# A two-layer transformer forward pass on one core: the norm between sublayers in three held steps, three late output tiles by stream, the softmax scaling inside the turning matmul, and one block's low part by an accumulating DMA

## The chip, the cores and the metric

The kernel runs on one core of one Trainium2 chip. The metric is device time in microseconds (us) of one execution; lower is better. Times of a kernel are given as the median of several runs with the lowest and the highest. A profiled execution gives the trace, with the start and the length of every instruction on the engines: PE (TensorE's matmuls), PEld (its weight loads), DVE (VectorE), ACT (ScalarE), POOL (GpSimd) and SP, which issues DMAs.

## The reference: what is computed

Two token streams of 256 tokens and width 1024, the latents and the context, go through two layers; in layer 1 the context serves only as keys and values, and the result is the latents alone. Cut to what matters:

```python
def _modulate(t, g, shift, scale):
    return _rms(t, g) * (1 + scale) + shift
def _swiglu(h, w13, w2):
    gte, up = jnp.split(h @ w13, 2, axis=-1)
    return (jax.nn.silu(gte) * up) @ w2
for i in range(2):            # layer 0 mixes by convolution, layer 1 by attention
    mod = (silu(c) @ mod_w[i] + mod_b[i])         # 9 vectors: shift, scale, gate of 3 sublayers
    lat = lat + 0.5 * gate * _swiglu(_modulate(lat, ...), ffn_w13[i, 0], ffn_w2[i, 0])
    y = _short_conv_mixer(h, ...) or _gqa_mixer(h, hc, ...)     # of the modulated norm
    lat = lat + gate * y
    lat = lat + 0.5 * gate * _swiglu(_modulate(lat, ...), ffn_w13[i, 1], ffn_w2[i, 1])
```

The hidden width of the ffn is 2816. Attention has 8 query heads and 2 key/value heads of width 128, with an RMS norm and a rotary embedding on queries and keys; 256 queries see 512 keys (context, then latents). The context stream goes through the same steps up to layer 1's keys and values. Everything is float32.

## The kernel before

**Layout.** Activations lie transposed: 8 tiles (`m` or `k`) of 128 features by 512 token columns, 256 of each stream (`S` = 256, `T2` = 512). `s` = 0 is the latents, `s` = 1 the context. A product keeps float32's accuracy by parts: `split` (line 91) makes a high part by an ACT copy to fp32r and a low part by a DVE subtraction, and `mm3` (112 to 118) issues three matmuls: high·high, high·low, low·high. Weights come as 1 MB tiles `wr` over SP's queue (`load_raw`, 86, three buffers), and are split into `wh` and `wl` (four buffers of 128x1024 each).

**Order.** A framework schedules each engine's instructions at build time by its own estimates and by the program's order, inserts the waits, and gives buffers from pools by name. An instruction passed through `tc.keep_in_program_order` stays, on its engine, behind everything that the program had written before it.

**FFN.** `ffn` (600) goes over the hidden tiles in three parts of 8, 7 and 7, and after each part `project` (454) multiplies by `w2` and adds to the residual `x` (`finish`, line 438, with the gate). Most column tiles of `w13` are done by `Pair` (525): a scheme of 7 block products in place of 8, in which the weight blocks A11, A12, A22 and the sums S1 to S4 meet the activations' blocks B and their sums T1 to T4 (`Blocks.sums`, 314). One pair is 7 products x 4 `k` x 3 matmuls = 84 matmuls of 256 columns. `head` does A11 and A12 (these need the first stream's norm only), `five`, `six`, `seven` and `four` the rest; `four` is the product of A22 with T4, whose weights are `w4h` and `w4l` (128x512, two buffers; split at line 561). In the first ffn of layer 0 some tiles are done plainly.

**The norm between sublayers.** `project` computes the output tiles in order; the last two (`late` = 2) are done for stream 0 first, then for stream 1, so that one stream's norm can run while the other is still being projected. `tail_norm` (386) runs with each tile: `square_add` (208) sums the squares; after the last tile `rms_inv` (226) sums over the partitions with four small matmuls (line 231), takes the root (ACT) and the reciprocal `ri` (DVE, line 240), and spreads it over the partitions with two 128x128 matmuls against the identity (line 242). Then `rest` makes the normed and modulated activations, first half of the features and then the second (lines 250, 304 and the split into `bh`, `bl`; or `norm_k` with `hh`, `hl` for a plain layout). These steps wait in a list, `pending`, and `flush` (381) runs them at places in the next stage's code. For stream 0 there are two steps, for stream 1 one, which also makes T1 to T4. The four projections with late tiles by stream are the ends of the first ffn of layer 0, of the convolution's `cw_out`, of the second ffn of layer 0, and of the first ffn of layer 1.

**The next stage after a norm** starts with stream 0: in `ffn` one plain tile's first 256 columns (`pg`, `pu`), the heads of two pairs (`p`, `q`), then the same tile's columns of stream 1. In the convolution (811 to 849) the first tile `m` = 0 goes by stream, 24 products each.

**Modulation.** The 18 x 8 tiles of the modulation vectors are dot products on DVE (`junk`, line 136: 128x1024 custom operations; 236 of them). They are done as filler: `tick(n)` (173) owes `n` units and issues whole ones, each 1 MB block of `modT` serving up to four; `mod_ready` (180) issues all that are still missing.

**Attention (908 to 1085).** `q_proj`, `k_proj` and `v_proj` with norms and the rotary part between; `scores` (1007) forms for each head two tiles of 128 queries by 512 keys, their maximum `mx`, the exponentials `e` with their sum (ACT, 1024), the reciprocal `r` (1028) and `pn` = e·r (DVE, 1032). `turn` (1036) transposes `pn` by matmuls against the identity (1041) and splits the result to `pth`, `ptl`; `mix` (1052) multiplies by the values. Then `project` with `wo`, the last norm, and the last ffn for the latents alone.

Of the kernel before, what the change touches and what calls it, by code (L numbers as in the profile page):

```python
# [39 lines left out]
def hybrid_kernel(ctx: ExitStack, tc: tile.TileContext, a: dict, out: bass.AP):  # L40
# [70 lines left out]

    def mm3(ps, w, m, first, last, more=False):
        wh, wl = w
        mh, ml = m
        kw = {"skip_group_check": True} if more else {}
        nc.tensor.matmul(ps, wh, mh, start=first, stop=False, **kw)  # L116
        nc.tensor.matmul(ps, wh, ml, start=False, stop=False, **kw)  # L117
        nc.tensor.matmul(ps, wl, mh, start=False, stop=last, **kw)  # L118
# [107 lines left out]
    def rms_inv(s, parts):  # L226

        pq = psmall("ss")
        for i in range(2):
            for n, t in enumerate(parts):  # L230
                nc.tensor.matmul(
                    pq[:, S + i : S + i + 1], t[:, i * P : i * P + P], ones[:, 0:1],
                    start=(n == 0), stop=(n == len(parts) - 1),
                )
# [5 lines left out]
        nc.vector.reciprocal(ri, rs)  # L240
        for i in range(2):
            nc.tensor.matmul(
                pq[:, i * P : i * P + P], ri[:, i : i + 1].to_broadcast([P, P]), ident,
                start=True, stop=True,
            )
# [38 lines left out]
    class Blocks:  # L284
# [29 lines left out]
        def sums(self):  # L314
# [8 lines left out]
            tt(out=b11, in0=b12, in1=b11, op=ALU.subtract)  # L323
            keep("T1", b11)
            tt(out=b12, in0=b22, in1=b12, op=ALU.add)
            tt(out=b22, in0=b22, in1=b11, op=ALU.add)
            keep("T2", b22)
            tt(out=b21, in0=b21, in1=b22, op=ALU.subtract)
            keep("T3", b12)
            keep("T4", b21)  # L330
# [50 lines left out]
    def flush(n=9):  # L381
        while pending and n:
            pending.pop(0)()
            n -= 1

    def tail_norm(l, j, h):
# [3 lines left out]
        def tail(m, c0, c1):  # L390
            square_add(m, c0, c1)
            if m == KT - 1:
# [5 lines left out]
                def inv():  # L398
                    return rms_inv(s, (accs[s], accs[s, "last"]))

# [8 lines left out]
                def both_parts():  # L409
                    ri = inv()  # L410
                    for part in range(2):
                        rest(part, ri)
                    if isinstance(h, Blocks):
                        h.sums()

                if s == 0:
                    keep = []

                    def one():
                        keep.append(inv())  # L420
                        rest(0, keep[0])

                    pending.append(one)
                    pending.append(lambda: rest(1, keep[0]))
                    if (l, j) == (1, 2):
                        flush()
                else:
                    flush()
                    pending.append(both_parts)
# [24 lines left out]
    def project(ws, src, nk, gate, tail, tot, late, ev, between=()):  # L454
# [42 lines left out]
        if late:  # L497

            wl = [get(m) for m in (6, 7)]
            if tail:  # L500
                ready()
            for s in range(2):
# [22 lines left out]
    class Pair:  # L525
# [6 lines left out]
        def __init__(self, src, h):  # L532
            self.h = h
            raw = load_raw(src)
            a21, a22, a11, a12 = (raw[:, i * T2 : i * T2 + T2] for i in range(4))
            tt = nc.vector.tensor_tensor
            sm = wp.tile([P, 2048], F32, name=nm("ws"), tag="ws", bufs=1)
            s1, s2, s3, s4 = (sm[:, i * T2 : i * T2 + T2] for i in range(4))
            self.w = {}

            def keep(keys, src):
                hi, lo = half()
                split(hi, lo, src)
                for i, key in enumerate(keys):
                    self.w[key] = [t[:, i * T2 : i * T2 + T2] for t in (hi, lo)]

            keep(("A11", "A12"), raw[:, 1024:])
            tt(
# [618 lines left out]
```

## Time and profile before

| what | value |
|---|---|
| median of 3 runs | 1613.26 us (1612.75 to 1616.25) |
| the profiled execution | 1611.37 us |
| its span in the trace | 1609.5 us |
| mean granted TensorE clock | 0.992 |
| DMA traffic | 248.77 MB |

How to read the rows. A group's row gives line, engine, operation, out<-in by the program's names, partitions x elements and type, the count, then busy us, mean ns of one, and the engine's idle time ahead of the group with what ended it. A row of the windows gives a stretch of time, then for each engine its busy us and the number of instructions that ran in it, the granted TensorE clock (1 is full speed), the mean busy share of the 16 DMA engines, and GB/s. A row of the waits gives engine, operation and line, what it waited for, the total, the number of times and the longest. A row of the timeline gives start and length; a wait stands in brackets. A row of the DMA issues gives the count, the size and the median time from issue to landing. TensorE's matmuls are pipelined, so the length of one is more than its share of the time; what a window holds tells the rate.

### The profile page before, as it was taken

Reading aid. Unit: us, or ns where it says so; the run is one execution under the profiler, and the core shown is the slowest. Engines: PE = TensorE matmul, PEld = TensorE weight load, DVE = VectorE, ACT = ScalarE, POOL = GpSimd, SP = SyncE. Lnnn points to the kernel's source line nnn. Section 1 sums busy time; section 2 is a strip of 40 time slices with the busy share of each in tenths; the row PEclk is TensorE's granted clock in tenths of the full one; section 3 lists DMA queues with packets and bytes.
Section 4 is the critical chain, followed back from the end, with each engine's and each line's share of the span. In section 5 each row is a group of like instructions: output and inputs, shape, how many; then the busy total and the mean of one; then the engine's idle time right before and its main releaser. Section 6 shows DMA issues by size and latency. Waiting matters only on the chain.

```text
span 1609.5 us, 25613 instructions
## 1 busy us (share of the span) xinstructions
PE 1576.1 (98%) x10566; PEld 1450.1 (90%) x10566; DVE 1332.4 (83%) x2035; ACT 722.2 (45%) x1110; POOL 0.2 (0%) x4
## 2 busy tenths in 40 slices
PE   9999999999999999999999999999999999899999
PEld 6788998999888889899899889889899897789999
DVE  4988778879998889799797999898898789965554
ACT  5532452544322365335255465245254455454443
POOL 0000000000000000000000000000000000000000
PEclk9999999999999999999999999999999999999999
DMA  8456235234565513353433413452432463755453
GB/s 320 162 183 209 80 122 180 90 135 152 177 221 186 180 41 117 132 183 100 168 120 115 154 54 131 172 195 96 156 129 96 180 214 108 270 201 185 169 194 109
DMA packets 38277, 248.77 MB, mean 155 GB/s; under 512 B 5136, under 2 KB 6928, under 8 KB 12304
## 3 DMA queue, kind: packets, MB, share of 16 engines
q1 hardware_dynamic: 35712, 245.38, 43.7%
q10 hardware_dynamic: 2448, 1.76, 0.4%
q8 instruction: 82, 1.34, 0.3%
q14 instruction: 35, 0.29, 0.1%
HBM read 244.77 MB, written 1.05 MB: 153 GB/s over the span
## 4 chain that ended last, share of the span: by engine, by line
PE 82%; DVE 12%; DMA 3%; ACT 2%; issue 1%; DVEq 0%; ACTq 0%; SPq 0%
PE py L117 7%; PE py L116 7%; PE py L118 7%; PE p L116 6%; PE p L118 6%; PE p L117 6%; PE q L118 5%; PE q L116 5%; PE q L117 5%; DVE junk L136 4%; DVE wl L93 3%; PE pg L117 2%; PE pg L118 2%; PE pg L116 2%; PE pu L117 2%; PE pu L118 2%
## 5 line engine op out<-in xcount | busy, mean ns | idle before, releaser
L92 ACT ACTIVATE wh<-wr 128x1024 fp32r<-128x1024 f32 (+2 forms) x274 | 274.4, 1014 | 395.0 <-PE py L117 108.7
L93 DVE TENSOR_TENSOR wl<-wr,wh 128x1024 fp32r<-128x1024 f32 (+2 forms) x274 | 318.2, 1167 | 97.0 <-ACT wh L92 96.4
L136 DVE CUSTOM_DVE_ANT_0 junk<-wr,scbc,modb 128x1024 bf16<-128x1024 f32 x236 | 302.5, 1282 | 39.6 <-DMA wr<-in_modT 37.0
L117 PE MATMUL py<-gl,wh 128*128 128x512 f32 (+1 forms) x746 | 263.2, 353 | 0.0
L116 PE MATMUL py<-gh,wh 128*128 128x512 f32 (+1 forms) x746 | 263.1, 353 | 0.0
L118 PE MATMUL py<-gh,wl 128*128 128x512 f32 (+1 forms) x746 | 262.9, 352 | 0.0
L93 DVE TENSOR_TENSOR wl<-ws,wh 128x1024 fp32r<-128x1024 f32 x112 | 136.8, 1223 | 27.3 <-ACT wh L92 27.0
L118 PEld LDWEIGHTS py<-gh,wl 128*128 128x128 f32 x746 | 141.1, 189 | 19.1
L116 PEld LDWEIGHTS py<-gh,wh 128*128 128x128 f32 x746 | 141.2, 189 | 18.6
L117 PEld LDWEIGHTS py<-gl,wh 128*128 128x128 f32 x746 | 141.2, 189 | 18.0
L92 ACT ACTIVATE wh<-ws 128x1024 fp32r<-128x1024 f32 x112 | 117.8, 1057 | 76.4 <-PE p L117 34.2
L116 PE MATMUL p<-th,wh 128*128 128x256 f32 x448 | 126.8, 283 | 0.0
L117 PE MATMUL p<-tl,wh 128*128 128x256 f32 x448 | 126.8, 283 | 0.0
L118 PE MATMUL p<-th,wl 128*128 128x256 f32 x448 | 126.6, 283 | 0.0
L117 PE MATMUL q<-bl,wh 128*128 128x256 f32 x336 | 95.2, 283 | 0.0
L116 PE MATMUL q<-bh,wh 128*128 128x256 f32 x336 | 95.1, 283 | 0.0
L118 PE MATMUL q<-bh,wl 128*128 128x256 f32 x336 | 95.1, 283 | 0.0
L438 DVE SCALAR_TENSOR_TENSOR x<-py,G,x 128x256 f32<-128x256 f32 x168 | 74.2, 480 | 21.4 <-PE py L118 21.2
L116 PEld LDWEIGHTS p<-th,wh 128*128 128x128 f32 x448 | 86.0, 192 | 0.5 <-ACT sg L584 0.2
L117 PEld LDWEIGHTS p<-tl,wh 128*128 128x128 f32 x448 | 86.0, 192 | 0.3
L118 PEld LDWEIGHTS p<-th,wl 128*128 128x128 f32 x448 | 85.9, 192 | 0.0
L116 PE MATMUL pg<-hh,wh 128*128 128x256 f32 (+1 forms) x240 | 75.8, 316 | 4.6 <-ACT hh L260 4.6
(236 smaller groups left out, 4001.3 us busy)
## 6 DMA issues: line engine op xcount, KB each, us to landing
wr<-in_w SPq DMA_DIRECT2D x88, 1024.0 KB, 4.9
wr<-in_modT SPq DMA_DIRECT2D x67, 1024.0 KB, 4.9
wr<-in_w2b SPq DMA_DIRECT2D x32, 896.0 KB, 4.6
wr<-in_w2a SPq DMA_DIRECT2D x16, 1024.0 KB, 4.9
wr<-in_cw_cx SPq DMA_DIRECT2D x8, 1024.0 KB, 4.9
wr<-in_mod SPq DMA_DIRECT2D x5, 1024.0 KB, 7.4
wr<-in_cw_b SPq DMA_DIRECT2D x4, 1024.0 KB, 4.8
wr<-in_cw_out SPq DMA_DIRECT2D x4, 1024.0 KB, 4.9
```

What stands on the lines that cost most here:

```text
L92: nc.scalar.activation(out=hi, in_=src, func=AF.Copy)
L93: nc.vector.tensor_tensor(out=lo, in0=src, in1=hi.bitcast(F32), op=ALU.subtract)
L116: nc.tensor.matmul(ps, wh, mh, start=first, stop=False, **kw)
L117: nc.tensor.matmul(ps, wh, ml, start=False, stop=False, **kw)
L118: nc.tensor.matmul(ps, wl, mh, start=False, stop=last, **kw)
L136: nc.vector.tensor_tensor_reduce(out=junk, in0=raw[:, j * D : j * D + D], in1=scbc[:, v, :], scale=1.0, scalar=modb[:, l, col : col + 1], ...
L438: nc.vector.scalar_tensor_tensor(out=x[:, m, s * S : s * S + S], in0=ps[:, o : o + S], scalar=g[:, m, s : s + 1], in1=x[:, m, s * S : s * ...
```

## The change

1. **The norm.** `rms_inv` becomes `rms_sum` (squares, root, reciprocal) and `rms_all` (the spreading). Their matmuls are pinned in program order (`held`), and so is the first matmul of the product that follows a flushed step (`pin`). Each stream queues three steps: `rms_sum`; `rms_all` with the first half; the second half. They are flushed one at a time: within the late tiles; in `ffn` after products k = 3 and k = 5 of the first tile and after the two heads; in the convolution after the 6th, 12th and 18th product of the first tile; in `q_proj(0)` at k = 6 (twice, once for each half of the columns). The last norm's steps, of the projection of `wo`, are flushed all at once, as before.
2. **Late tiles.** Three instead of two output tiles go by stream in the four projections.
3. **Sums in steps.** `Blocks.sums` and the sums of a `Pair` are cut into numbered steps; after a norm they are issued in turn behind the heads.
4. **A22's low part.** The DVE subtraction goes. ACT writes the high part and, from it, its negative; a DMA issued by GpSimd adds the weights from HBM.
5. **Softmax.** `pn` goes. DVE makes `dr` = identity·r (128x128), and `turn` multiplies e by `dr`, which transposes and scales in one float32 matmul.
6. **The pace of the modulation.** In q/k/v the ticks go from 1, 1, 2 to 3, 4, 4, 3, 3; the tick of 2 per head goes; in the projection of `wo` 0.6 per tile instead of 1.

The diff, cut:

```diff
     def mm3(ps, w, m, first, last, more=False):
...
-        nc.tensor.matmul(ps, wh, mh, start=first, stop=False, **kw)
+        i = nc.tensor.matmul(ps, wh, mh, start=first, stop=False, **kw)
+        if pin[0]:
+            tc.keep_in_program_order(i)
+            pin[0] = False
...
-    def rms_inv(s, parts):
+    def held(ins):
+        return tc.keep_in_program_order(ins)
+
+    def rms_sum(s):
...
+    def rms_all(pq, ri):
...
-        def sums(self):
+        def sums(self, n):
...
-                if s == 0:
-                    keep = []
-
-                    def one():
-                        keep.append(inv())
-                        rest(0, keep[0])
-
-                    pending.append(one)
-                    pending.append(lambda: rest(1, keep[0]))
-                    if (l, j) == (1, 2):
-                        flush()
-                else:
+                keep = []
+
+                def spread():
+                    keep.append(rms_all(*keep.pop()))
+                    rest(0, keep[0])
+
+                if s:
                     flush()
-                    pending.append(both_parts)
+                pending.extend(
+                    (lambda: keep.append(rms_sum(s)), spread, lambda: rest(1, keep[0]))
+                )
+                if (l, j) == (1, 2):
+                    flush()
...
             for s in range(2):
-                for i in range(2):
+                for i, m in enumerate(ms):
                     ps = psum("py")
-                    products(ps, wl[i], range(nk // 2), s * S, s * S + S)
-                    flush(1)
-                    products(ps, wl[i], range(nk // 2, nk), s * S, s * S + S)
-                    finish(6 + i, ps, s * S, s * S + S, gate, tail)
+                    products(ps, wl[i], range(cut), s * S, s * S + S)
+                    if i:
+                        flush(1)
+                    products(ps, wl[i], range(cut, nk), s * S, s * S + S)
+                    if i == 0:
+                        flush(1)
+                    finish(m, ps, s * S, s * S + S, gate, tail)
...
-            split(*self.w["A22"], a22)
+
+            nc.scalar.activation(out=hi, in_=a22, func=AF.Copy)
+            nc.scalar.activation(out=lo, in_=hi.bitcast(F32), func=AF.Copy, scale=-1.0)
+            nc.gpsimd.dma_start(out=lo, in_=self.src[:, T2:1024], accum_op=ALU.add)
...
-                    w13_mm(pp, w, h, range(KT), 0, S)
-                    flush()
+                    w13_mm(pp, w, h, range(4), 0, S)
+                    flush(1)
+                    w13_mm(pp, w, h, range(4, 6), 0, S)
+                    flush(1)
+                    w13_mm(pp, w, h, range(6, KT), 0, S)
                     for i in (1, 2):
                         heads.append(Pair(a["w13"][l, b, i], h))
                         heads[-1].head()
+                        flush()
+                    h.sums(0)
+                    heads[0].sums(0)
+                    h.sums(1)
+                    heads[0].sums(1)
+                    h.sums(2)
+                    heads[1].sums(0)
                     w13_mm(pp, w, h, range(KT), S, T2)
                     w13_post(pp, gs[0], 0, T2)
+                    heads[1].sums(1)
...
-                gate, tail if end else None, tot, 2 if end and tot == T2 else 0, ev, between,
+                gate, tail if end else None, tot, 3 if end and tot == T2 else 0, ev, between,
...
-            if qt == 0:
-                pn2 = hot("pn", F32)
-            pn = pn2[:, qt * T2 : qt * T2 + T2]
-            nc.vector.tensor_scalar(out=pn, in0=e, scalar1=r, scalar2=None, op0=ALU.mult)
-            r_.append(pn)
+            dr = ap.tile([P, P], F32, name=nm("dr"), tag="dr", bufs=6)
+            nc.vector.tensor_scalar(out=dr, in0=ident, scalar1=r, scalar2=None, op0=ALU.mult)
+            r_.append((e, dr))
...
-                nc.tensor.transpose(
-                    pt[:, kt * P : kt * P + P], pn[qt][:, kt * P : kt * P + P], ident
+                e, dr = pn[qt]
+                nc.tensor.matmul(
+                    pt[:, kt * P : kt * P + P], e[:, kt * P : kt * P + P], dr,
+                    start=True, stop=True,
```

Counted over the whole changed program, 87 matmuls of 512 columns become 174 of 256; DVE has 56 instructions fewer for A22, ACT as many more, and GpSimd issues 56 DMAs of 128x512.

More of the change, by code (lines that the diff above doesn't have):

```diff
@@ L224, in square_add @@
                     accs[s, "last"] = part
-    def rms_inv(s, parts):
+    def held(ins):
+        return tc.keep_in_program_order(ins)
+    def rms_sum(s):
         pq = psmall("ss")
+        parts = accs[s], accs[s, "last"]
         for i in range(2):
             for n, t in enumerate(parts):
-                nc.tensor.matmul(
+                held(nc.tensor.matmul(
                     pq[:, S + i : S + i + 1], t[:, i * P : i * P + P], ones[:, 0:1],
                     start=(n == 0), stop=(n == len(parts) - 1),
-                )
+                ))
         rs = tp.tile([P, 2], F32, name=nm("rs"), tag="rs")
@@ L912, in q_proj @@
             for k in range(KT):
+                if p == 0 and k == 6:
+                    flush(1)
                 mm3(
@@ L993, in hybrid_kernel @@
     pq.append(q_proj(3))
+    tick(3)
     q_rope(2, pq[2])
@@ L998, in hybrid_kernel @@
     v_proj(0)
+    tick(3)
     q_rope(3, pq[3])
```

111 lines of the change are left out of this document (58 added, 53 removed).

## Prediction

> **What bounds the kernel now.** I read the page first, then the windows of the trace, then TensorE's waits, then the order of instructions around the longest of them.
>
> ```profile
> span 1609.5 us, 25613 instructions
> PE 1576.1 (98%) x10566; PEld 1450.1 (90%) x10566; DVE 1332.4 (83%) x2035; ACT 722.2 (45%) x1110; POOL 0.2 (0%) x4
> PE 82%; DVE 12%; DMA 3%; ACT 2%; issue 1%; DVEq 0%; ACTq 0%; SPq 0%
> ```
>
> The reader is to see that TensorE bounds the kernel nearly everywhere: it is busy in 98% of the span and is 82% of the chain that ended last. But "busy" counts a matmul that runs at a low clock or waits inside itself as work, so the loss has to be read from how many matmuls a window holds. Columns below: window, length, then busy us and count of PE, PEld, DVE, ACT, POOL, granted clock, DMA share, GB/s.
>
> ```profile
> 390.00:395.00 5.00, 4.81 (x36) 4.24 (x35) 4.66 (x13) 3.57 (x7) 0.00 (x0) 1.00 0.07 30
> 500.00:520.00 20.00, 20.00 (x90) 16.58 (x89) 17.19 (x29) 5.23 (x6) 0.00 (x0) 1.00 0.57 204
> 580.00:600.00 20.00, 16.48 (x111) 15.53 (x111) 18.92 (x22) 14.51 (x21) 0.00 (x0) 0.83 0.00 1
> 915.00:920.00 5.00, 4.26 (x37) 4.06 (x35) 5.00 (x10) 3.43 (x7) 0.00 (x0) 1.00 0.49 162
> 920.00:940.00 20.00, 17.91 (x135) 17.31 (x135) 17.19 (x33) 14.48 (x30) 0.00 (x0) 0.91 0.20 68
> 940.00:960.00 20.00, 18.47 (x134) 17.53 (x133) 18.70 (x21) 13.14 (x18) 0.00 (x0) 0.91 0.17 54
> 1060.00:1065.00 5.00, 3.96 (x29) 3.34 (x27) 5.00 (x9) 2.90 (x5) 0.00 (x0) 1.00 0.42 123
> 1065.00:1070.00 5.00, 4.46 (x37) 4.46 (x38) 5.00 (x6) 1.59 (x3) 0.00 (x0) 1.00 0.45 182
> 1440.00:1460.00 20.00, 20.00 (x169) 20.00 (x168) 11.68 (x15) 9.82 (x16) 0.00 (x0) 1.00 0.53 184
> ```
>
> Two windows set the scale: 90 matmuls of 512 columns fill 20 us (0.222 us each), or 169 of 256 columns (0.118 us each, 42 in 5 us). The other windows hold 256-column products and lie at four places. At three of them one sublayer ends and the next norm must be ready: T1 (390, into the convolution), T2 (580, into the second ffn) and T3 (915 to 960, layer 0 into layer 1). The fourth, T3b (1060), lies inside layer 1's first ffn, with DVE busy in all of its 10 us. Their lost time, by missing matmuls:
> - T1: (42 − 36) × 0.118 = 0.7 us there, and about as much just behind it: 1.4.
> - T2: (169 − 111) × 0.118 = 6.8 us.
> - T3: (5 + 34 + 35) × 0.118 = 8.7 us.
> - T3b: (13 + 5) × 0.118 = 2.1 us.
>
> Their sum is 19 us, and it is most of what the change can win outside attention. What T2's loss is made of:
>
> ```profile
> 574.27 1.23 DVE L93 TENSOR_TENSOR bl<-hr,bh 128x1024 fp32r<-128x1024 f32 x1 [0.67 <-ACT bh L92]
> 575.41 0.16 DVE L240 RECIPROCAL ri<-rs 128x2 f32<-128x2 f32 x1
> 578.30 0.60 PE L242 MATMUL ss<-ident,ri 128*128 128x128 f32 x4
> 578.95 2.05 DVE L250 SCALAR_TENSOR_TENSOR t<-x,A,ss 128x256 f32<-128x256 f32 x5 [2.26 <-PE ss L242]
> 582.15 1.06 ACT L92 ACTIVATE bh<-hr 128x1024 fp32r<-128x1024 f32 x1
> 583.25 0.58 PE L116 MATMUL pg<-bh,wh 128*128 128x256 f32 x1 [3.03 <-ACT bh L92]
> 585.57 0.41 PE L116 MATMUL pg<-bh,wh 128*128 128x256 f32 x1
> 585.78 0.41 PE L117 MATMUL pg<-bl,wh 128*128 128x256 f32 x1
> ```
>
> The reciprocal of the root is ready at 575.6, yet the two matmuls that spread it (L242) stand behind products until 578.3: 2.7 us are given away by the order alone. From L242 to the first product that needs its result it takes 583.25 − 578.30 = 4.95 us, and only 1.8 us of products stand between. So TensorE waits 3.03 us, and afterwards it runs at half speed for a while: products 0.21 us apart at 585.6, clock 0.83 in the window. That slow clock is the other half of the 6.8 us.
>
> **The change part by part.** The profiled execution took 1611.37 us, 1609.5 of them span; the median of the runs is 1613.26, 1.9 us more. I sum against 1611.4 and add 1.9 at the end.
>
> *The norm in three held steps, three late tiles.* Three late tiles by stream replace two, in four projections. In the changed order 96 products of 256 columns stand at T2 between the last product of the projection and the first that needs the second stream's norm, where 72 stand before: 11.5 us of cover against 8.6 (12.2 and 9.3 with the small matmuls between). The spreading matmuls stand 6.3 us behind the last projection product, against 7.8. With the 4.95 us from there, bh is ready at 11.3 under 12.2 of cover, and the 3.03 us wait goes with the slow clock that follows it. What is late next is DVE: the second half's bl, the sums and then tl of the blocks are now issued in turn behind the heads (one 128x1024 operation is 1.2 us by the rows above), and DVE was 18.9 of 20 us busy in that window. I leave 1.5 us for that: T2 −5.3. T3 has the same new order, with a fuller DVE: I leave 2.2 of 8.7: −6.5. T1's steps move up from one flush at its 12th product to three: −1.0. T3b has no norm; its one long wait (q for wl, 1.3 us, in the rows below) goes if DVE gets the 0.69 us per pair that the third part takes off it, twice before that wl: −1.3. Behind each held matmul stands TensorE's whole queue, so a reciprocal that is late by x costs x; at T2 it had 2.7 us to spare.
>
> ```profile
> PE pg L116 <- ACT hh L260: 4.6, 2, 2.8
> PE ss L231 <- ACT sq L214: 1.7, 2, 1.2
> PE q L118 <- DVE wl L93: 1.3, 1, 1.3
> PE ss L242 <- DVE ri L240: 1.8, 2, 1.5
> PE pt L1041 <- DVE ptl L93: 2.2, 1, 2.2
> ```
>
> The 4.6 us of pg behind hh (waits of TensorE over the span; total, times, longest) belong to the last norm, into layer 1's second ffn. Its steps are flushed all at once before and after the change, so I leave them. The waits of ss (1.7 and 1.8 us in four places) are the price that a held step can have, and a bound for a new one: 1.5 us.
>
> On the clock, the Trainium skill's page "TensorE: Matmul & The Clock Gate", section "What's actually happening", says that the clock is halved after an idle window of some 3.4 us and comes back after as long a busy one. T2's row agrees (3.0 us idle, 0.83); T3's rows do not quite, since the longest wait there is ss for sq, 1.2 us, and the clock still fell to 0.91. By the page's rule, waits of 1 to 2 us would leave the clock alone and the sum would be some 2 us lower; by T3's rows they can cost half as much again.
>
> *The splitting.* One product of 512 columns becomes two of 256: 29 × 3 = 87 fewer of the one, 174 more of the other: 174 × 0.118 − 87 × 0.222 = +1.2 us.
>
> *Block A22's low part.*
>
> ```profile
> L93 DVE TENSOR_TENSOR w4l<-wr,w4h 128x512 fp32r<-128x512 f32 x56 | 38.4, 687 | 0.0
> L92 ACT ACTIVATE w4h<-wr 128x512 fp32r<-128x512 f32 x56 | 35.1, 627 | 59.9 <-PE p L117 43.3 <-DMA wr<-in_w 16.5
> wr<-in_w SPq DMA_DIRECT2D x88, 1024.0 KB, 4.9
> out_lat<-x SPq DMA_DIRECT2D x8, 128.0 KB, 1.7
> ```
>
> DVE loses 56 × 0.69 = 38 us, ACT gains 56 × 0.63 = 35 us, and GpSimd issues 56 DMAs of 256 KB that add the weights to the negated high part. ACT is 45% busy, so it has room. GpSimd's queue is empty before, so nothing is queued behind these. In steady state DVE is not the bound, so of the 38 us only T3b's 1.3 show; the rest is part of what keeps DVE's backlog at T2 and T3 as small as I took it. For the DMA no row exists. Its nearest are a store of 128 KB, 1.7 us to landing, and a load of 1024 KB, 4.9 us; the accumulate must also read its destination, so up to twice the load, 9.8. One pair takes 7 × 12 products × 0.118 = 9.9 us; with two buffers a buffer's turn is 19.9 us, less 1.4 for its own 12 products and some 5 for ACT's queue leaves about 13.5. Either end of 1.7 to 9.8 is under that: cost nothing. I take 3 us, near the store.
>
> *Attention.*
>
> ```profile
> 1256.00:1334.00 78.00, 77.54 (x536) 71.62 (x535) 69.77 (x133) 39.63 (x67) 0.00 (x0) 1.00 0.54 193
> 1334.00:1380.00 46.00, 38.18 (x245) 32.87 (x245) 44.68 (x111) 26.44 (x60) 0.00 (x0) 0.93 0.32 115
> 1380.00:1413.00 33.00, 26.54 (x207) 25.00 (x206) 32.07 (x55) 16.57 (x26) 0.00 (x0) 0.98 0.89 315
> L136 DVE CUSTOM_DVE_ANT_0 junk<-wr,scbc,modb 128x1024 bf16<-128x1024 f32 x236 | 302.5, 1282 | 39.6 <-DMA wr<-in_modT 37.0
> L93 DVE TENSOR_TENSOR wl<-wr,wh 128x1024 fp32r<-128x1024 f32 x198 | 241.0, 1222 | 70.0 <-ACT wh L92 69.5
> L1032 DVE TENSOR_SCALAR pn<-e,r 128x512 f32<-128x512 f32 x16 | 7.6, 483 | 0.0
> L78 DVE MEMSET ones<- 128x128 f32 x1 | 0.2, 165 | 0.8 <-PEq L1154 0.8
> L1041 PE MATMUL pt<-ident,pn 128*128 128x128 f32 x64 | 10.3, 297 | 3.7 <-DVE ptl L93 2.2 <-ACT e L1024 0.9 <-DVE a L93 0.4
> 1323.56 1.95 PE L970 MATMUL kri<-ident,rq 128*128 128x128 f32 x16
> 1325.26 0.36 PE L116 MATMUL pv<-wh,hh 128*128 128x256 f32 x1
> ```
>
> The three windows are q/k/v, scores to mix, and wo. In the last two DVE is the bound (44.7 of 46, 32.1 of 33 us). By the changed order: in q/k/v 18 units of the modulation (junk) instead of 10, so DVE 69.8 + 8 × 1.28 = 80.0 us; that becomes its length with a little idle, 80.5: **+2.5**. In the middle, 7 units instead of 12 (−6.4), four low parts of wo instead of one (+3.7), and 16 scalings that go from 128x512 to 128x128, 0.483 to about the memset's 0.165 us (−5.1): DVE 44.7 − 7.8 = 36.9. TensorE gains work: the transposes have one record each for 64 instructions; the fp32 matmuls of L970 are 8 instructions with 16 records, and they fill 1325.26 − 1323.56 = 1.70 us, 0.106 per record. So 64 × 0.106 = +6.8 us. Its 38.2 us at clock 0.93 are some 35.5 of work; with 6.8 it is 42.3. Both engines depend on each other, so 42.5: **−3.5**. In wo, three low parts fewer and a lighter pace of units: 33 − 3 × 1.22 = 29.3, TensorE 26.5; with the wait for the tail 30.5: **−2.5**. Together −3.5. The order also puts nine of the modulation's blocks (1024 KB each) ahead of wv on SP's queue, where two stood. The ends of the three windows together: +10 (the 8 units show in full, nothing is won behind them) and −8 (q/k/v hides its units, and the two others run at TensorE's and DVE's work alone).
>
> **Sum.** −1.0 − 5.3 − 6.5 − 1.3 + 1.2 + 0 − 3.5 = −16.4: 1595.0 for the profiled scale, and 1596.9 against the median.
>
> **The rivals.**
> - *DVE's backlog takes the place of the norm wait.* For it: DVE has 18.9, 17.2 and 18.7 us of 20 in T2's and T3's windows and 5.0 of 5 in T3b's, and bl already shows as a wait. Against it: the sums of the blocks are now cut into steps and 0.69 us per pair is gone. Half of T2's and T3's gain stays away: −16.4 + 5.9 = −10.5, 1602.8.
> - *q/k/v becomes bound by its loads.* The 8 units cost more than their DVE time because wq and wv wait for a buffer of raw weights behind modulation blocks; for it: junk already waited 37.0 us for in_modT over the kernel; against it: DMA share is 0.54 there. q/k/v +8 instead of +2.5, attention nothing won: −16.4 + 5.5 + 3.5 = −7.4, 1605.9.
> - *Slower: the accumulating DMA is late in every pair.* Its place is the 56 blocks A22; if landing takes d us with d over 13.5, each pair grows by (d − 13.5)/2, since two buffers share the wait. That is 56 × 0.5 = 28 us per us of d: from d = 13.5 + 16.4 / 28 = 14.1 on the whole gain is gone, and at d = 15 the time is 1597 + 1.5 × 28 = 1639. Against it: the nearest landings are 1.7 and 4.9 us. For it: DVE works 83% of the time beside GpSimd, and no row shows how GpSimd issues there. The Trainium skill's page "SBUF — State Buffer", in its box on the "DVE blocks DMA" trap, says that DMAs issued from GpSimd can wait while DVE holds a port that both share; no run here shows it yet, and by it d would grow with DVE's longest unbroken work.
> - *Better:* T2 and T3 lose nothing at all, since short waits leave the clock full: −16.4 − 3.7 = −20.1, 1593.2; with attention's three windows at −8 for −3.5, 1588.7.
>
> **How the numbers follow.** Forecast 0.46, backlog 0.20, loads 0.17, late DMA 0.12, better 0.05. About 0.2% (3.2 us) is what a measurement of this kernel can tell from no change. All of the forecast, the better case, nearly all of the backlog (0.19) and two thirds of the loads (0.11) are faster by more: 0.81. Slower are the late DMA's 0.12; 0.07 remain within. The likeliest case alone is 1590 to 1602. The range takes in backlog and loads, up to the worse end of attention with half a backlog (1596.9 + 10 + 3.5 = 1610.4, cut to 1609), and below the better case with 3.7 us for what the windows' counts may miss at T1 to T3: 1585 to 1609.
>
> **What would show it.** Right: in T2's and T3's windows over 155 matmuls of 256 columns per 20 us and a clock over 0.95; pg's wait for bh gone; the spreading matmuls less than 7 us behind the projection. In attention, 128 records of the turning matmul, DVE under 40 us between the first maximum and the last a, q/k/v near 80 us. The accumulating DMA lands in under 8 us, and no product p waits for w4l. Wrong: waits of p or q for tl, th or w4l; a wait of pv or pq for its weights; DVE full at T3 with a low clock.

## The result, and the profile after

The change made the kernel slower: 1630.05 us median (1627.55 to 1631.55, 4 runs) against 1613.01 us (1611.66 to 1616.25); the ratio is 1.0101 with a 95% interval of 1.0082 to 1.0121. That is 17 us more where 16 us less were forecast.

First the page of the changed kernel: span, engines, the chain by engine, and the new DMA.

```profile
span 1628.2 us, 26070 instructions
PE 1591.4 (98%) x10717; PEld 1470.4 (90%) x10717; DVE 1301.8 (80%) x1979; ACT 750.9 (46%) x1170; POOL 49.1 (3%) x60
...
PE 86%; DVE 9%; ACT 3%; issue 1%; DMA 1%; ACTq 0%; DVEq 0%
...
w4l<-in_w POOLq DMA_DIRECT2D x56, 256.0 KB, 5.0
```

TensorE's share looks the same, 98%, and VectorE has 31 us less to do. The page does not show where 19 us of span went. What shows it is a table of stretches, cut at matmuls that both kernels have: the first and the last `py` of each projection, the last `pv` and the last `pav` (start times in the two traces; a stretch that is not listed differs by 0.5 us at most).

| stretch | before | after | difference |
|---|---|---|---|
| start to the first projection | 127.1 | 128.8 | +1.7 |
| convolution (T1 at its start) | 134.3 | 137.4 | +3.1 |
| T2 to the next projection | 87.9 | 85.1 | −2.8 |
| after that projection, to the second one | 67.9 | 69.9 | +2.0 |
| last projection of layer 0 and T3, to the next | 133.0 | 129.6 | −3.4 |
| that projection and T3b behind it | 116.5 | 122.8 | +6.3 |
| q/k/v: last `py` to last `pv` | 57.1 | 73.6 | +16.5 |
| attention: last `pv` to last `pav` | 41.1 | 40.2 | −0.9 |
| from there to the end of wo's projection | 26.4 | 22.1 | −4.3 |

They add to +18.2, all but half a microsecond of the spans' difference. T2 and T3 did gain, and so did wo; the rest took it back two and a half times over.

The windows of the changed kernel (columns as in the prediction), first at T2, T3 and T3b, then through q/k/v, attention and wo:

```profile
585.00:605.00 20.00, 16.65 (x131) 15.82 (x131) 19.78 (x22) 14.81 (x21) 0.00 (x0) 1.00 0.04 7
920.00:940.00 20.00, 19.00 (x159) 18.77 (x159) 15.30 (x32) 14.32 (x31) 0.86 (x1) 1.00 0.46 131
940.00:960.00 20.00, 16.63 (x131) 15.80 (x130) 19.77 (x21) 14.81 (x22) 0.00 (x0) 1.00 0.05 10
1060.00:1065.00 5.00, 2.85 (x15) 2.11 (x13) 4.96 (x10) 1.59 (x3) 0.00 (x0) 1.00 0.59 205
1065.00:1070.00 5.00, 4.22 (x21) 4.02 (x20) 5.00 (x6) 2.05 (x4) 0.88 (x1) 0.54 0.70 215
1289.00:1310.00 21.00, 18.91 (x124) 18.09 (x123) 18.08 (x38) 11.07 (x23) 0.00 (x0) 0.84 0.33 115
1310.00:1330.00 20.00, 18.59 (x105) 16.55 (x103) 17.72 (x30) 6.83 (x11) 0.00 (x0) 0.91 0.73 244
1330.00:1355.00 25.00, 20.02 (x138) 19.44 (x137) 20.53 (x33) 9.64 (x14) 0.00 (x0) 0.80 0.78 273
1355.00:1403.00 48.00, 46.44 (x336) 42.52 (x335) 45.20 (x115) 28.94 (x64) 0.00 (x0) 1.00 0.35 130
```

T2 now holds 131 matmuls in 20 us at full clock, and T3's two windows hold 159 and 131. So 38 are still missing at T2 (some 4.5 us) and 48 at T3 (some 5.7 us), with VectorE at 19.8 of 20 us in the two windows of 131. T3b has become worse (15 and 21 in 5 us, where 42 fit). And in q/k/v neither TensorE nor VectorE is full, so something else holds them up. TensorE's waits over the span name it:

```profile
PE pq L118 <- ACT wh L92: 3.6, 2, 3.1
PE p L122 <- DVE tl L93: 2.7, 2, 1.4
...
PE p L118 <- ACT wh L92: 2.2, 1, 2.2
...
PE pc L118 <- ACT hh L273: 0.8, 2, 0.4
```

The wait of `pg` for `bh` (3.0 us before) is gone; `tl` of the blocks stands in its place. New are waits for `wh`, the high part of weights, in q/k/v (`pq`) and at T3b (`p`). The DMA issues on SP's queue, around q/k/v, before the change and after it (start, length from first to last, count):

```profile
1274.81 0.33 SPq L88 DMA_DIRECT2D wr<-in_modT  x1
1289.35 0.33 SPq L88 DMA_DIRECT2D wr<-in_wq  x1
1291.85 0.33 SPq L88 DMA_DIRECT2D wr<-in_modT  x1
1294.22 0.33 SPq L88 DMA_DIRECT2D wr<-in_wq  x1
1308.43 0.33 SPq L88 DMA_DIRECT2D wr<-in_wv  x1
```

```profile
1285.09 25.87 SPq L88 DMA_DIRECT2D wr<-in_modT  x4
1315.61 0.33 SPq L88 DMA_DIRECT2D wr<-in_wq  x1
1319.22 6.26 SPq L88 DMA_DIRECT2D wr<-in_modT  x2
1326.36 0.33 SPq L88 DMA_DIRECT2D wr<-in_wq  x1
1334.69 0.33 SPq L88 DMA_DIRECT2D wr<-in_modT  x1
1338.11 0.33 SPq L88 DMA_DIRECT2D wr<-in_wv  x1
```

The issues stand in the program's order. Four blocks of the modulation now stand ahead of the third wq; each needs one of three raw buffers, and a buffer comes free when VectorE has done with it. So the four take 25.9 us to issue; two of the waits, 22.3 us together, are for VectorE's low part `wl` of earlier weights. The third wq is asked for at 1315.6, 26.7 us behind the end of the projection (1288.9); before it was 7.5 us (1289.35 against 1281.9).

### The profile page after: what moved, and what is told of

Same layout as the page of the kernel before. It is cut to its first block, busy times and chain, and to the rows that moved or that the text cites. A ratio compares the mean times of both kernels' runs of the same rounds, so it can differ in the third digit from the quotient of the medians.

```text
span 1628.2 us, 26070 instructions
## 1 busy us (share of the span) xinstructions
PE 1591.4 (98%) x10717; PEld 1470.4 (90%) x10717; DVE 1301.8 (80%) x1979; ACT 750.9 (46%) x1170; POOL 49.1 (3%) x60
## 3 DMA queue, kind: packets, MB, share of 16 engines
q1 hardware_dynamic: 35712, 245.38, 42.8%
## 4 chain that ended last, share of the span: by engine, by line
PE 86%; DVE 9%; ACT 3%; issue 1%; DMA 1%; ACTq 0%; DVEq 0%
PE py L118 9%; PE py L122 9%; PE py L123 9%; PE p L123 7%; PE p L118 6%; PE p L122 6%; PE q L118 5%; PE q L123 5%; PE q L122 5%; DVE junk L141 4%; PE pg L118 2%; PE pg L123 2%; PE pg L122 2%; PE pu L118 2%; PE pu L122 2%; PE pu L123 2%
## 5 line engine op out<-in xcount | busy, mean ns | idle before, releaser
L118 PE MATMUL py<-gh,wh 128*128 128x512 f32 (+1 forms) x767 | 267.2, 348 | 0.0
L122 PE MATMUL py<-gl,wh 128*128 128x512 f32 (+1 forms) x767 | 266.6, 348 | 0.0
L123 PEld LDWEIGHTS py<-gh,wl 128*128 128x128 f32 x767 | 145.0, 189 | 19.8 <-DVE wl L93 1.4
L118 PEld LDWEIGHTS py<-gh,wh 128*128 128x128 f32 x767 | 145.3, 189 | 17.5
L122 PEld LDWEIGHTS py<-gl,wh 128*128 128x128 f32 x767 | 145.4, 190 | 17.4
L580 POOL DMA_DIRECT2D w4l<-in_w x56 | 48.9, 874 | 1189.9 <-ACT w4l L579 611.6
```

The source lines that it names most:

```text
L118: i = nc.tensor.matmul(ps, wh, mh, start=first, stop=False, **kw)
L580: nc.gpsimd.dma_start(out=lo, in_=self.src[:, T2:1024], accum_op=ALU.add)
```

## The experiments

The theories. **A**: q/k/v is long because the modulation's blocks hold up the loads of wq and wv (its rival A2: because of VectorE's time for their units). **C**: T1 is lost by the pinned products. **D**: the losses behind T2 and T3 are units forced in one burst. Rivals throughout: the accumulating DMA is late, or TensorE's added work shows. Each run has its own runs of the kernel before beside it on its chip, so ratios are compared; "stretch" is a row of the table above, from the profiled execution. It scatters by 1 to 2 us at the transitions (T2 has 85.1 and 86.5 us with the same code in the changed kernel and in e1) and by up to 3 at the start: e2, whose code is that of the kernel before up to q/k/v, takes 130.2 us to the first projection, against 127.1. So the +1.7 there is not shown to come from the change.

**e1: the old pace.** The changed kernel, with the ticks as before:

```diff
-    tick(3) ... tick(4) ... tick(4) ... tick(3) ... tick(3)     # q/k/v
+    tick(1) ... tick(1) ... tick(2)
+        tick(2)                                                 # per head
-    S, 0, 0.6,
+    S, 0, 1,
```

> The changed kernel with its sixth part undone: the modulation's pace in q/k/v, attention and wo as before (ticks 1, 1, 2 in q/k/v, 2 per head, 1 per tile of wo). Theory A (the units' blocks stand ahead of wq and wv in SP's queue and hold the three raw buffers, so TensorE waits for its weights in q/k/v): the 14 us that q/k/v's products now last longer mostly come back, attention gives back 2 to 3 of its 3.5 us: 1630 becomes 1615 to 1620. Theory B (the loss is elsewhere: the accumulating DMA, TensorE's added work, the held steps): 1626 to 1630.

1623.14 us, ratio 1.0053 (1.0032 to 1.0074) where the whole change has 1.0101. In the gap between the two theories' ranges: q/k/v's stretch falls from 73.6 to 60.7 us, but wo's goes back from 22.1 to 25.5, and its profiled execution was longer at T2, T3 and T3b, by 4.4 us together.

**e2: the pace alone**, on the kernel before.

> The kernel before with the sixth part alone (the new pace). Theory A: q/k/v lasts some 14 us longer, attention and wo win 3 to 5: 1613 becomes 1621 to 1626. Theory B: 1610 to 1615.

1620.10 us, ratio 1.0029 (1.0019 to 1.0039): slower, a little under A's range. q/k/v 57.1 to 68.3, attention 41.1 to 40.3, wo 26.4 to 22.9. The sixth part alone costs some 5 us net.

**e3: the same units behind the loads.** All 17 are owed after the first v product:

```diff
-    tick(3) ... tick(4) ... tick(4) ... tick(3)
     v_proj(0)
-    tick(3)
+    tick(17)
```

> The changed kernel with the same 17 units in q/k/v, but all owed at one place, behind the load of wv and the first v product, so that no block of the modulation stands between the loads of wq, wk and wv. Theory A (the order of the loads): q/k/v's products have their weights again, and wait no longer than before for them; the units' 22 us of VectorE then stand ahead of the scores and give part back: 1616 to 1624. Theory A2 (not the loads but the units' time on VectorE): 1628 to 1634.

1632.75 us, ratio 1.0117 (1.0100 to 1.0134): no gain, as A2 had it. Yet the stretches say more than the total. q/k/v is back at 61.3 us, and attention, which now starts with the burst, lasts 53.0 instead of 40.2:

```profile
1351.50:1404.50 53.00, 42.43 (x276) 36.08 (x275) 51.39 (x124) 28.39 (x61) 0.00 (x0) 0.90 0.52 183
```

VectorE is full there (51.4 of 53.0 us). The run cannot tell loads from units, since it moved both; e13 and e14 do.

**e13 and e14: units without loads, loads without units.** e13 leaves out the loads that q/k/v would issue for the modulation and lets their units work on a resident vector; e14 keeps the loads and cuts each of those units to 16 of its 1024 columns. In both, a part of the modulation values is not computed from its own block or columns.

```diff
-            raw = load_raw(a["modT"][l, ch * 4 + pair])
+            raw = None if cheap[0] else load_raw(a["modT"][l, ch * 4 + pair])     # e13
-            out=junk,
+            out=junk[:, : 16 if cheap[0] else D],                                # e14
```

> The changed kernel, in which the modulation blocks that would be loaded during q/k/v are left out: their units work on a resident vector instead (these modulation values are then not the reference's), so VectorE has the same 17 units and SP's queue only the weights. If the loads' place in the queue and the raw buffers make q/k/v long (73.6 us from the last product of the projection to the last v product; 60.7 with the old pace): 59 to 63. If VectorE's units do: 70 to 74.

> The changed kernel with all blocks loaded as before, but each unit in q/k/v cut to 16 columns (values again not the reference's): SP's queue and its order stay, VectorE loses some 17 x 1.2 us. If only the queue's order and the transfers matter: 68 to 74. If the blocks hold the raw buffers because VectorE comes to them late: 59 to 64.

Single runs, without an interval: e13 1618.76 us and e14 1626.48 us, beside 1612.34 of the kernel before. q/k/v lasts 63.5 us without the loads and 69.1 without the units' time, against 73.6. So the loads cost some 10 us and the units' time some 4: theory A holds for most of it. These are differences of single executions, each with one thing removed, and they need not add: the new pace as a whole costs 12.9 us there (e1). SP's issues in e13, then the four blocks in e14:

```profile
1287.14 11.47 SPq L88 DMA_DIRECT2D wr<-in_wq  x2
1311.64 0.33 SPq L88 DMA_DIRECT2D wr<-in_wv  x1
```

```profile
1286.32 25.83 SPq L88 DMA_DIRECT2D wr<-in_modT  x4
```

In e13 both wq are issued within 11.5 us. In e14 the four blocks still take 25.8 us, as in the changed kernel, though their units take next to no time: the buffers are held by the weights ahead of them, until VectorE has made their `wl`, and hardly by the units.

**e4: A22's low part by VectorE** again, in the changed kernel.

```diff
-            nc.scalar.activation(out=hi, in_=a22, func=AF.Copy)
-            nc.scalar.activation(out=lo, in_=hi.bitcast(F32), func=AF.Copy, scale=-1.0)
-            nc.gpsimd.dma_start(out=lo, in_=self.src[:, T2:1024], accum_op=ALU.add)
+            split(hi, lo, a22)
```

> The changed kernel with its fourth part undone: A22's low part by the VectorE subtraction as before, no accumulating DMA. If the DMA is hidden, as its 5.0 us to landing say: 1629 to 1634, the upper end if the 38 us that VectorE takes over lengthen T2, T3 and T3b. If the DMA is late (the rival of the prediction): below 1625.

1630.82 us, ratio 1.0101 (1.0084 to 1.0119): the same as the whole change. The DMA is hidden, as 5.0 us to landing said, and the 38 us that VectorE saves show nowhere: T2, T3 and T3b are 85.1, 86.5 and 75.1 us with it as without.

**e5: no pinned product in the convolution and in q/k/v**, on e1.

```diff
-                if n in (5, 11, 17):
-                    flush(1)
+                if n == 11:
+                    flush()
+                    pin[0] = False
...
-                if p == 0 and k == 6:
-                    flush(1)
```

> The changed kernel with the old pace (as e1_pace_back), and in the convolution and in q/k/v the context's norm steps flushed all at once at the old places, with no pinned product behind them. Theory C (a pinned product holds pv and pb back while pc, which is not pinned, runs through all of k and meets hh that are not ready; in q/k/v the held sum waits for its square): the convolution's stretch goes from 137.4 back to 134.5 us, q/k/v's from 60.7 to 57.5: 1623 becomes 1616 to 1618. Rival (three late tiles or VectorE's load are the cause): 1622 to 1624.

1621.88 us, ratio 1.0040 (1.0025 to 1.0054), against e1's 1.0053. The total falls by some 2 us, less than expected, and the intervals overlap; the stretches moved: convolution 137.4 to 135.2, q/k/v 60.7 to 58.5. The timeline of TensorE in the changed kernel shows what the pin does:

```profile
393.94 0.28 PE L118 MATMUL pc<-hh,wh 128*128 128x256 f32 x1
...
394.88 0.38 PE L118 MATMUL pc<-hh,wh 128*128 128x256 f32 x1 [0.42 <-ACT hh L273]
...
397.24 0.39 PE L118 MATMUL pc<-hh,wh 128*128 128x256 f32 x1 [0.42 <-ACT hh L273]
398.23 0.39 PE L123 MATMUL pb<-hh,wl 128*128 128x256 f32 x1 [0.60 <-DVE wl L93]
398.79 0.28 PE L240 MATMUL ss<-ones,acc 128*128 128x1 f32 x2
```

From 393.3 to 397 TensorE issues `pc` alone: the next product of `pv` is the pinned one and stays behind the held sum (398.8), and `pb` waits for its weights (`wl`), while `pc` may run ahead, reaches its last k without the products of `pv` and `pb` between, and meets `hh` that ACT is still making. The waits are short (the three shown and one of 0.25 us for `hl`), and behind them the clock is slow in the changed kernel, but not in e7 (described below), which has the same pins, the same order and the same waits. The windows of the two:

```profile
400.00:410.00 10.00, 10.00 (x74) 10.00 (x73) 8.08 (x20) 3.58 (x9) 0.00 (x0) 0.84 0.56 210
```

```profile
400.00:410.00 10.00, 10.00 (x86) 10.00 (x85) 9.67 (x23) 4.59 (x9) 0.00 (x0) 1.00 0.56 210
```

So the convolution takes 135.9 us in e7 with the pins and 135.2 in e5 without: the order alone costs some 0.7 us. The rest of the 2.2 us goes with the slow clock, which most of the profiled executions with the pins show (e4 has 0.75 in this window, and its convolution takes 139.0 us).

**e6: two late tiles**, on e1.

```diff
-                gate, tail if end else None, tot, 3 if end and tot == T2 else 0, ev, between,
+                gate, tail if end else None, tot, 2 if end and tot == T2 else 0, ev, between,
...                              # and 2 instead of 3 in the projection cw_out
```

> e1_pace_back with two late tiles by stream instead of three (the second part undone). If the gain of T2 and T3 (2.8 and 2.7 us between the projections) came from the longer cover: it goes, less 1.1 us of splitting: 1624 to 1629. If it came from the order of the held steps alone: 1621 to 1623.

1624.74 us, ratio 1.0059 (1.0044 to 1.0074), e1's within the intervals. Gains and losses cancel. T2 goes to 88.9 us (e1: 86.5, the whole change: 85.1, before: 87.9): its gain comes from the third late tile, and the held steps alone win nothing. T3 with its projection goes to 132.1 (131.1, 129.6, 133.0), which is within the scatter. q/k/v, which the fourth of these projections leads into, grows from 60.7 to 67.4 us; TensorE waits there for the norm's results (1280 to 1362 us):

```profile
PE pq L122 <- DVE hl L274: 2.4, 2, 1.6
PE pq L118 <- ACT hh L273: 2.2, 2, 1.4
```

In e1 these waits are 0.3 and 0.8 us. On the other side the stretch behind T2 goes back from 69.8 to 67.9 and that behind T3 from 124.3 to 116.0, so the third late tile also makes those losses; the convolution, 137.4 to 135.6, runs at full clock.

**e7: the sums in one piece**, on e1: `sums` of both pairs right behind their making, those of the blocks together behind the second flush.

> e1_pace_back with the sums of the blocks and of the two first pairs made in one piece each, as before (the third part undone). If the steps keep VectorE's backlog small: T2 and T3 lose 2 to 4 us each, 1627 to 1631. If not: 1621 to 1625.

1622.34 us, ratio 1.0048 (1.0031 to 1.0065), e1's within the intervals: cutting the sums is worth nothing that shows. T2 is 85.4 and T3 86.7 us; the wait has only changed its name, from `tl` and `wh` back to `bl` and `bh`. TensorE's waits at T2 (575 to 605 us) in e7 and in the changed kernel:

```profile
PE pg L122 <- DVE bl L93: 1.5, 2, 1.3
PE pg L118 <- ACT bh L92: 0.6, 1, 0.6
```

```profile
PE p L122 <- DVE tl L93: 1.3, 1, 1.3
PE q L118 <- ACT wh L92: 0.9, 1, 0.9
PE pg L122 <- DVE bl L93: 0.7, 1, 0.7
PE q L118 <- ACT th L92: 0.4, 1, 0.4
```

**e8: units earlier**, on e1: 7 per tile instead of 6 in the convolution, 3.2 instead of 1.7 in the second projection of layer 0's second ffn.

```diff
-        tick(6)
+        tick(7)
...
+                3.2 if (l, b, t) == (0, 1, 1) else ev, between,
```

> e1_pace_back with 8 units of the modulation more in the convolution (7 per tile instead of 6) and 12 more in the second projection of layer 0's second ffn (3.2 per tile instead of 1.7). Theory D (what is lost in the stretches behind T2 and T3, 2.0 and 6.1 us, are units that the gates force there in one burst, ahead of the load of w13 in SP's queue): these stretches go back to 67.9 and 70.3 us, 1623 becomes 1615 to 1618, at most 2 us more in the convolution. Rival (the cut sums or the accumulating DMA delay the first pair there): 1622 to 1625.

1621.36 us, ratio 1.0037 (1.0024 to 1.0050). Behind T2 the stretch is back at 67.9 us (from 69.8), behind T3 at 114.1 (from 124.3), better than before. But behind the projection that got the 12 units it grew from 67.9 to 77.6: the stall went where the burst went. SP's issues there, in e8 and in the kernel before (their projections end at 816.3 and 812.6):

```profile
797.87 9.13 SPq L88 DMA_DIRECT2D wr<-in_modT  x3
812.52 16.48 SPq L88 DMA_DIRECT2D wr<-in_w  x4
```

```profile
781.34 13.21 SPq L88 DMA_DIRECT2D wr<-in_modT  x2
798.22 21.53 SPq L88 DMA_DIRECT2D wr<-in_w  x5
```

With three blocks in place of two, the first w13 of the next third is asked for 3.8 us ahead of the projection's end instead of 14.4. The total is above theory D's range, since the stall moved instead of going, but the stretches show D's mechanism.

**e9: the third late tile owes its units**, on e1. The loop over late tiles calls no `tick`; one more late tile in four projections therefore owes 1.5 to 1.7 units less each. VectorE had done 164 units when the projection behind T3 began, 160 after the change; the gate of that ffn needs all units of its chapter and forces what is missing in that projection. The load of w13 stands behind them; SP's issues of it in the changed kernel and in the kernel before:

```profile
1056.33 23.60 SPq L88 DMA_DIRECT2D wr<-in_w  x5
```

```profile
1050.35 31.66 SPq L88 DMA_DIRECT2D wr<-in_w  x6
```

The projection ends at 1061.9 and 1059.7, so w13 is asked for 5.6 us ahead of that instead of 9.4, and `p` then waits 2.2 us for `wh` (in the waits above).

```diff
             wl = [get(m) for m in ms]
+            tick(ev * (late - 2))
```

> e1_pace_back with one line more: the third late tile owes its units of the modulation (1.5 to 1.7) as the tile had done before the change; the loop over late tiles calls no tick. Theory D2 (four projections owe 1.5 to 1.7 units less each, so the gate of the next ffn finds some 4 units missing and forces them in one burst ahead of the load of w13): behind T2 69.8 goes back to 67.9 us, behind T3 76.4 to 70 and 47.9 to 46.2: 1623 becomes 1613 to 1616, unless the units cost as much at T2 and T3 (rival: 1620 to 1624).

1619.94 us, ratio 1.0029 (1.0020 to 1.0038), against e1's 1.0053. Behind T2 67.9 us, behind T3 116.0 (46.2 and 69.8), as D2 said, and w13 is asked for 9.4 us ahead again. T3 itself took back 3.5 us (88.0 to 91.5) in the profiled execution, and the total is above D2's range, at the edge of the rival's: the stall behind is gone, but a part of what the units cost has moved. TensorE's waits at T3b (1055 to 1075 us) in e9:

```profile
PE q L123 <- DVE wl L93: 0.7, 1, 0.7
PE q L118 <- ACT wh L92: 0.2, 1, 0.2
```

**e10 and e12: the parts that help, together.** e10 is e5 with e7's sums, 7 units per tile in the convolution and 2.1 per tile in layer 0's second ffn; e12 has 2.4, 1.7 and 2.1 there.

> What the runs point to, together: three late tiles, old pace in q/k/v, attention and wo, context steps flushed at the old places in convolution and q/k/v (e5), sums in one piece (e7), and units owed earlier: 7 per tile in the convolution and 2.1 instead of 1.7 per tile in layer 0's second ffn. If the parts add: 1622 − 7 (e5) − 1.5 (first ffn) − 2 − 7 (behind T2 and T3) − 2 (wo) = 1605 to 1610, against some 1615 of the kernel before on the same chip; if 2.1 per tile stalls the loads as 3.2 did: 1613 to 1620.

> e10_best with the units of layer 0's second ffn owed by projection at 2.4, 1.7 and 2.1 per tile instead of 2.1 in all three. If the 3.6 us that e10 lost behind the second projection (71.5 against 67.9 us) came from its own higher pace, they go and the stretch behind T3 stays at 46.2 and 67.9: 1613 becomes 1608 to 1611, 0.2 to 0.4 per cent under the kernel before. If the units now burst elsewhere: 1612 to 1616.

e10: 1612.83 us, ratio 0.9993 (0.9982 to 1.0004). e12: 1612.82 us, ratio 0.9990 (0.9980 to 0.9999). The parts did not add: both only reach the kernel before. e12 has the stretch behind the second projection at 67.9 us again (e10: 71.5) but loses 2.9 us in the projection ahead of T3 (46.0 against 43.1) and 2.6 in q/k/v (61.1 against 58.5). Nor does the softmax's gain (e11, next) show here: attention and wo together take 68.4 us in e10, 67.5 in the kernel before and 64.4 in e11. In e10 the first wo is asked for 4.0 us ahead of the last `pav`, in e11 8.0 us, and in e10 `py` waits 2.5 us for wo's `wh`; why the load comes later there is open.

**e11: the softmax alone**, on the kernel before: the fifth part as in the diff of the change.

> The kernel before with the fifth part alone (scaling in the turning matmul). If attention is bound by VectorE, as its 44.7 of 46 us said: 5 us of VectorE's work go, 1611 to 1614 against 1615. If the 6.8 us more of TensorE's work show: 1617 to 1622. If attention follows the chain from score to turned tile on both engines: 1614 to 1617.

1610.17 us, ratio 0.9980 (0.9969 to 0.9991): 0.2 per cent faster than the kernel before, just under the first range. Of the two parts that were run alone this one gains and the pace (e2) loses; the other four were not run alone. The windows from the last v product to wo's first product, in the kernel before and in e11:

```profile
1339.00:1380.00 41.00, 33.18 (x204) 27.87 (x203) 39.68 (x100) 23.00 (x53) 0.00 (x0) 0.92 0.34 125
```

```profile
1339.40:1376.50 37.10, 35.98 (x259) 32.57 (x258) 36.04 (x98) 22.64 (x53) 0.00 (x0) 1.00 0.38 138
```

VectorE's 39.7 us become 36.0, and the stretch gets 3.9 us shorter with it. TensorE's 64 added records, 6 us more busy time (16.1 against 10.3 us in the groups of the turning matmul), fill what were idle gaps, and the clock that had been granted at 0.92 is 1.00.

## Why the prediction was wrong, point by point

Two steps failed above all: the length of q/k/v, and what the third late tile takes along besides its matmuls.

- *What bounds the kernel* was read rightly, and so were T1, T2, T3 and T3b as the places where TensorE loses time.
- *T2 −5.3 and T3 −6.5*: right in sign, half in size: −2.8 and −3.4 (with its projection). The wait for `bh` went, as worked out; I had left 1.5 and 2.2 us for what VectorE does late, and some 4.5 and 5.7 us are missing there. The rival of VectorE's backlog put the two at half, in part by luck: of the 3.3 us of TensorE's waits at T2, 2.0 are for VectorE (`tl`, `bl`) and 1.3 for ScalarE (`wh`, `th`), and giving VectorE its 38 us of work back moved neither place (e4). The slow clock of T2 went as forecast (1.00 for 0.83). At T2 the third late tile made the gain (e6); the held steps and the cut sums made none that shows (e6, e7).
- *T3b −1.3, and nothing behind T2*: +6.3 and +2.0 instead. **One step that failed is that the third late tile was costed by its matmuls alone.** A late tile calls no tick, so its units moved into the burst that the next gate forces, in front of w13's loads (e9 takes away the +2.0 and all of the +6.3; e8 makes and unmakes the stall elsewhere). The 0.69 us per pair that part four takes off VectorE (the prediction says the third part), which I had counted on there, changed nothing (e4).
- *T1 −1.0*: +3.1, of which 2.2 go with the pin (e5): some 0.7 are its order and the rest a slow clock behind it, which e7 does not show. The other 0.9 is open. I had asked what stands behind a held matmul, and not what may overtake it.
- *Splitting +1.2*: the last projection of the first ffn is longer by 0.3 us (42.8 to 43.1), and four times that would be the term. But with two late tiles and the held steps e6 has 43.0 there, so the runs do not tell the splitting from the held steps.
- *A22 0*: right. The DMA lands in 5.0 us, between the bounds of 1.7 and 9.8, and e4 shows it hidden. GpSimd's issue took 0.87 us each. The Trainium skill's page "SBUF — State Buffer", in its box on the "DVE blocks DMA" trap, warns of a port that VectorE and GpSimd share; whether it has a part in the 5.0 us no run here shows, and no product waits for `w4l`.
- *q/k/v +2.5*: +16.5, **the step that failed by most: the text took VectorE's busy time (80.0 us) as the stage's length and put the loads' wait at nothing.** It had counted nine blocks ahead of wv where two stood (the trace has seven), but gave their wait no price in the sum. The rival of the loads had the mechanism, wq and wv behind modulation blocks, with a chance of 0.17 and at +8, half of its size. By the runs: some 10 us the loads, 4 the units' time on VectorE (e13, e14), and some 2 the pinned steps (e5). The price of a place in SP's queue here is not the transfer but the wait for a raw buffer, 25.9 us for four blocks. Attention and wo give a part back, so by the totals the pace costs 5 us alone (e2) and some 8 in the changed kernel (1.0101 against 1.0053); the rest of the 17 us lies at T1, behind T2, at T3b and in the pinned steps of q/k/v.
- *Attention −3.5*: −0.9 with the new pace, since the old pace's units there cost little (e1: 40.6 us). *wo −2.5*: −4.3. The fp32 matmul's price was about right (64 records; 5.8 us in e11, 6.8 forecast), and hidden.

## What to carry to other kernels

Filler work has a place in every queue that it uses: before its pace is changed, or a loop is entered that does not call it, follow its loads through the issuing queue and its buffers, and ask which weights stand behind them. A pinned instruction holds back what is written behind it, but not what can overtake it; the order that results has to be read instruction by instruction. And where a change has six parts, price each part's side effects in the loop that it shortens, since here the two parts that were run alone had opposite signs, and the third late tile won at one end of a stage what it lost at the other.

## What the runs showed of the hardware that was not expected

The clock does not follow from the length of a wait alone. Two windows with the same wait of `pg` for `hh` in the first ffn (2.8 us before, 2.7 after):

```profile
60.00:70.00 10.00, 7.22 (x32) 5.59 (x31) 10.00 (x21) 6.75 (x13) 0.00 (x0) 1.00 0.58 211
```

```profile
60.00:70.00 10.00, 7.28 (x25) 5.53 (x25) 8.93 (x19) 5.05 (x11) 0.00 (x0) 0.83 0.58 211
```

The first is the kernel before, the second the changed one: 1.00 and 0.83, seven matmuls of 0.222 us or 1.6 us apart, about what the +1.7 us ahead of the first projection is. At T2 and T3 after the change waits of up to 1.4 us left the clock at 1.00, while waits of 0.25 to 0.6 us in the convolution were followed by 0.84, and the same waits in e7 by 1.00. The Trainium skill's page "TensorE: Matmul & The Clock Gate", section "What's actually happening", says that the window over which activity is judged runs freely; the rows agree with that. A slow stretch behind a short wait would then in part be a matter of when it falls, which no run here varied by itself.
